# Two edits to a hybrid decoder layer on one core: when g's scale is copied, and when w_out's scale and first split are made

## The chip, the core and the metric

The kernel runs on one core of a Trainium2 chip. The metric is the device time of one launch in microseconds. Five engines work side by side, each through its own instructions in a fixed order: PE (matrix products; its weight loads are shown as PEld), DVE (VectorE), ACT (ScalarE), POOL (GpSimd) and SP, which here only issues transfers (DMA).

## What is computed

One layer (DEPTH 1, 1024 positions, width 1024) of a parallel-branch hybrid block:

```python
h = rms_norm(x, norm_mix_pre)
q, k, v, cb, cc, cx, g_att, g_conv = split(h @ w_in)
y_att  = stick_breaking_attention(q, k, v) @ w_att_branch     # 8 heads of 64
y_conv = (cb * causal_dwconv(cc * cx)) @ w_conv_branch
m = sigmoid(g_att) * y_att + sigmoid(g_conv) * y_conv
x = x + rms_norm(m @ w_out, norm_mix_post)
h = rms_norm(x, norm_ffn_pre)
a, g = split(causal_dwconv(h @ w_up))                          # width 2816 each
x = x + rms_norm((gelu(g) * a) @ w_down, norm_ffn_post)
```

## The kernel before

All products take float16 operands. A float32 tensor is scaled by a power of two and then split: ACT writes the rounded high part, DVE the remainder as the low part (`split`, L100: ACT at L102, DVE at L103). A product is then three passes on PE, high by high, high by low, low by high (PASSES, L38). The power of two for a weight comes from the sum of its squares: ACT squares each tile (`sumsq`, L62), DVE adds up the partial sums and rounds the total (L75, L76), PE adds over the partitions with a product by a matrix of ones (L81), and DVE makes the scale and its inverse by integer arithmetic on the exponent (L83 to L86). `scale_of` (L65) does all of this after the squares, and `wsplit` (L124) is `scale_of` followed by one `split` for each tile.

The work goes in stages: (1) the start, where x is normed, transposed and multiplied by w_v; (2) the attention, with the other input products filling PE's time beside it; (3) the branch products and seven blocks of gates, d = 1 to 7; (4) the product with w_out, with the second norm between its tiles; (5) the feed-forward part.

**The start** (L441 to L776) is ordered by hand-made means: jobs with costs in microseconds are handed to a planner (`Plan`, L2128), which simulates PE, ACT, DVE, POOL and SP with these costs and emits each engine's instructions in the order found. PE jobs marked `seq` keep the order in which they are written; other jobs go where the simulation has them ready. The jobs that matter here:
- The gain g of the first norm arrives as one row. DVE takes its maximum and a power of two from it (L476, L199 to L202) and rounds the pair (L481). PE spreads the row over the partitions in two halves (`gpb`, L496) and then the pair (`ps2`, L498). DVE copies the pair into `gs` (L500); its first entry is `s_h`, the scale of h.
- `norm_halves` (L511) norms a tile of 128 positions in two halves of 512 columns: squares on ACT (L514) and DVE (L516), small DVE operations (L518, L519), the power -1/2 on POOL (L521), then on DVE one product for each half (L523). It runs for tile 0 and for tile 1.
- On PE in written order: 4 products that only keep it busy (`warm`, L489), the transposes of tile 0 in two halves (L535), 2 more `warm`, two raw products of tile 0 with w_v (`v_raw`, L602, float32 without split, eight in all, k = 0 to 7), the transposes of tile 1 (`turn_pe(1)`, L543), the other six raw products.
- ACT scales the transposed tile 0 by `s_h` into `h32` (L711), which the raw products take; it also makes the high part of the transposed tile 1 (L725; the low part is DVE's L726) and squares w_v, whose scale is needed for its split (L729, L731). PE's product for that scale is L588.

**The gates** (L1281 to L1306): block d multiplies h by two columns of w_in, with seven half-size products in place of eight (`Gates`, a `Pair`, L2345). `prod(i)` (L2361) is 12 matrix products of 512 columns; three accumulators (banks a, b, c) take the seven, and each is evicted by ACT or DVE right after a `prod` (L2383). The written order of a block is `prod(1)`, the previous block's `prod(4)`, the preparation of the next block's weights, `merge_m` of the previous block (L1246), then `prod` 6, 5, 2, 7, 3, with `split_m` of the previous block behind 5. Stage 3 has no order by hand: the framework's scheduler goes through it with its own timing and takes for each engine the instruction that is ready and stands first in the program, evictions ahead.

At the end of block 5 the eight tiles of w_out are fetched and squared (`wfetch`, L1306). Behind the loop stand `gp[7].prod(4)` (L1307), `wsplit` for w_out (L1308), the merge and the split of block 7 (L1309, L1310). Raw tiles and split tiles of w_out, the `y` tiles of the branches, the gates' `ug`, and the split m of blocks 4 to 7 all come from one pool of 16 slots (`slab`, L251).

**The product with w_out** (`out_proj`, L1499; PE at L1510) starts with two tiles at once, k outermost: for each of the eight k it takes 2 tiles x 2 halves x 3 passes = 12 products. So w_out's tile k is needed 12 k products after the first. This stage and the feed-forward part are ordered by a second planner run (L1392), whose inputs the change does not touch.

Of the kernel before, what the change touches and what calls it, by code (L numbers as in the profile page):

```python
# [18 lines left out]
F32 = mybir.dt.float32  # L19
# [5 lines left out]
P = 128  # L25
T = 1024
D = 1024
KD = D // P
# [16 lines left out]
class Layer:  # L45
# [76 lines left out]
        return sm, st  # L122

    def wsplit(self, name, sm, st, pools=None):  # L124

        nc = self.nc
        wh, wht = (pools or (self.ws, "ws", self.wh, "wh"))[2:]
        s, inv = self.scale_of(sm, len(st), keep=len(st) > 1)
        out = []
        for i, t in enumerate(st):  # L130
            w = wh.tile([P, 2, D], F16, tag=wht, name=f"wh_{name}_{i}")
            if name[:2] in self.pool_split:
                nc.gpsimd.tensor_scalar(t, t, s, 0.0, ALU.mult, ALU.add)
                nc.scalar.activation(w[:, 0, :], t, AF.Copy)
                nc.gpsimd.tensor_tensor(w[:, 1, :], t, w[:, 0, :], ALU.subtract)
            else:
                self.split(w, t, s, f"{name}_{i}")
            out.append(w)
        return out, inv

    def wload(self, name, srcs, pools=None, after=None):
# [138 lines left out]
    def mixer(self, mid):  # L280
        tc, nc, a = self.tc, self.nc, self.a
        hT = self.hp.tile([P, 2, KD, T], F16, tag="hT", name="hT")
        with ExitStack() as ph1:
# [64 lines left out]
            with tc.tile_pool(name="ptp", bufs=2, space=bass.MemoryType.PSUM) as ptp:  # L348
# [75 lines left out]
                st = [self.ws.tile([P, D], F32, tag="ws", name=f"ws_v_{i}") for i in range(4)]  # L424
# [13 lines left out]
                gs = self.small("g_pre", keep=True)  # L438
                cst = self.small("cst", keep=True)
                inv_ov = cst[:, 1:2]  # L440
                with tc.manual_schedule(engines={ET.PE, ET.DVE, ET.Activation, ET.SP, ET.Pool}):  # L441
                    pl = Plan(dict(s=12, ws=4, wh=8, pm=3, pt=2, sm=8, rb=8, sc=16))
                    pl.own, pl.loaded = {"PE": 0.0}, 22.0
                    vec, act, pe, pool = nc.vector, nc.scalar, nc.tensor, nc.gpsimd
                    NOTE = lambda: Buf(None, lambda: {})

                    def given(p, tile, avail=0.0):
                        b = Buf(p, None)
                        b.tile, b.avail = tile, avail
                        pl.caps[p] -= 1  # L450
                        return b

                    def V(cost, fn, r, w, **kw):
                        return pl.add("V", cost, fn, r, w, **kw)

                    def A(cost, fn, r, w, **kw):
                        return pl.add("A", cost, fn, r, w, **kw)
# [9 lines left out]
                    raw_v = [given("ws", st[i], (6.1, 8.7, 10.0, 11.5)[i]) for i in range(4)]  # L467
                    sv = given("sm", self.small("sm_v"))
                    hb = [NOTE() for _ in range(8)]
                    jv = Buf("s", lambda: self.slot([P, D], F32, "jk_v_2"))  # L470
                    g_s, g_c, g_t = NOTE(), NOTE(), NOTE()
                    h0, h1 = slice(0, NH), slice(NH, D)
# [13 lines left out]
                    def warm(n):  # L486
                        def f():
                            for _ in range(n):
                                pe.matmul(wm.t, wz[:, :P], wz, start=True, stop=True)  # L489
                        M(0.43 * n, f, [zero], [wm])  # L490
# [3 lines left out]
                    ps2 = Buf("pm", lambda: pm.tile([P, NH], F32, tag="pm", name="g2"))  # L494
                    for c in range(2):
# [1 line left out]
                                                      gr[0:1, ds(c * NH, NH)], start=True, stop=True), [one_row, g_row], [(gpb, str(c))])  # L497
                    M(0.3, lambda: pe.matmul(ps2.t[:, 0:2], self.ones[0:1, :], g_c.t["g16"][0:1], start=True, stop=True),  # L498
                      [g_c], [ps2])
                    V(0.15, lambda: vec.tensor_copy(gs[:, 3:5], ps2.t[:, 0:2]), [ps2], [g_s])  # L500
                    def norm(tt):
                        r, x = Buf("sm", lambda: self.small(f"r_pre{tt}")), xs[tt]
                        A(1.25, lambda: self.sumsq(xt[tt], r.t[:, 0:1], f"n_pre{tt}"), [x], [r])
                        V(0.15, lambda: vec.tensor_scalar(r.t[:, 1:2], r.t[:, 0:1], 1.0 / D, EPS, ALU.mult, ALU.add), [], [r])
                        pl.add("G", 0.6, lambda: pool.tensor_tensor(r.t[:, 2:3], r.t[:, 1:2], self.neghalf, ALU.pow), [], [r])
                        g = gpb if tt < 2 else gbb
                        V(1.28, lambda: vec.scalar_tensor_tensor(
                            xt[tt], xt[tt], r.t[:, 2:3], g.t.rearrange("p k t -> p (k t)") if tt < 2 else gb,
                            ALU.mult, ALU.mult), [r, g], [x])

                    def norm_halves(tt):  # L511
                        r, x = Buf("sm", lambda: self.small(f"r_pre{tt}")), xs[tt]
                        lo, hi = xt[tt][:, :NH], xt[tt][:, NH:]
                        A(0.82, lambda: act.activation(self.junk(f"jk_n_pre{tt}")[:, :NH], lo, AF.Square, accum_out=r.t[:, 0:1]),  # L514
                          [(x, "0")], [(r, "0")])
                        V(0.76, lambda: vec.scalar_tensor_tensor(jv.t[:, :NH], hi, 1.0, hi, ALU.mult, ALU.mult,  # L516
                                                                 accum_out=r.t[:, 3:4]), [(x, "1")], [(r, "1"), jv])
                        V(0.15, lambda: vec.tensor_scalar(r.t[:, 4:5], r.t[:, 3:4], 1.0 / D, EPS, ALU.mult, ALU.add), [], [(r, "1")])  # L518
                        V(0.15, lambda: vec.scalar_tensor_tensor(r.t[:, 1:2], r.t[:, 0:1], 1.0 / D, r.t[:, 4:5], ALU.mult, ALU.add),  # L519
                          [(r, "0"), (r, "1")], [(r, "2")])  # L520
                        pl.add("G", 0.6, lambda: pool.tensor_tensor(r.t[:, 2:3], r.t[:, 1:2], self.neghalf, ALU.pow), [], [(r, "2")])  # L521
                        for c, sl in enumerate((slice(0, NH), slice(NH, D))):
                            V(0.66, lambda sl=sl: vec.scalar_tensor_tensor(  # L523
                                xt[tt][:, sl], xt[tt][:, sl], r.t[:, 2:3], gpb.t.rearrange("p k t -> p (k t)")[:, sl],
                                ALU.mult, ALU.mult), [(r, "2"), (gpb, str(c))], [(x, str(c))])

                    pt = {}

# [60 lines left out]
                        V(0.45, post, [ps], [b])  # L589
                        return b  # L590

                    h32 = Buf("s", lambda: self.slot([P, KD, P], F32, "h32"))
                    own = hT[:, :, :, :P]
                    pv = {}

                    def v_bank(tt):
                        pv[tt] = Buf("pm", lambda: pm.tile([P, NH], F32, tag="pm", name=f"pv{tt}"))
# [103 lines left out]
                        vec.tensor_scalar(cst[:, 1:2], inv_h, bv.t["inv"], 2.0 ** 15, ALU.mult, ALU.mult)  # L701

                    warm(4)
                    norm_halves(0)
                    turn_halves(0)
                    warm(2)
                    norm_halves(1)
                    v_bank(0)
                    square_v(0, 0, slice(0, D), "A")
                    for c in range(2):  # L710
# [6 lines left out]
                    square_v(3, 5, h1, "V")  # L717
                    bv = total("v", sv, lambda: sv.t, 6)
                    V(0.15, lambda: vec.tensor_scalar(vs0.t[:, 0:1], bv.t["s"], 2.0 ** -15, None, ALU.mult), [bv], [vs0])
                    for k in range(2):  # L720
                        v_raw(k)
                    turn_pe(1)
                    for k in range(2, KD):
                        v_raw(k)
                    A(1.1, lambda: act.activation(hT[:, 0, :, ds(P, P)], pt[1].t, AF.Copy, scale=s_h), [pt[1], g_s], [(hb[1], "0")])  # L725
                    V(1.27, lambda: vec.scalar_tensor_tensor(hT[:, 1, :, ds(P, P)], pt[1].t, s_h, hT[:, 0, :, ds(P, P)],  # L726
# [408 lines left out]
            with tc.manual_schedule(engines={ET.PE, ET.DVE, ET.Activation}):  # L1135
# [52 lines left out]
                for name, t in wtasks.items():  # L1188
                    if any(o.eng == "sum" for o in t.ops):
# [3 lines left out]
                        st = next(o.st for o in t.ops if o.st)  # L1193
# [17 lines left out]
        with ExitStack() as ph2:  # L1211
# [29 lines left out]
            def branches(*ds_, bi=1):  # L1241
                for d in ds_:
                    for _ in branch(bi, d, pm):
                        pass
# [9 lines left out]
            def split_m(d, m):  # L1254
                t = self.o16p.tile([P, 2, T], F16, tag="o16", name=f"m16_{d}") if d < 4 else \
                    self.slot([P, 2, T], F16, f"m16_{d}")
                self.split(t, m, s_m, f"m{d}")
                m16.append(t)
# [21 lines left out]
            wo_pools = (self.slab, "s", self.slab, "s")  # L1280
            for d in range(1, 8):  # L1281
                p = gp[d]
                p.prod(1)
                if d > 1:
                    gp[d - 1].prod(4)
                if d < 7:
                    self.pair_split(f"g{d + 1}")
                    self.pair_fetch(f"g{d + 2}" if d < 6 else "u0")
                if d > 1:
                    ms.append(merge_m(d - 1))  # L1290
                for i in (6, 5, 2, 7, 3):
                    p.prod(i)
                    if d >= 4 and i == 5:
                        split_m(d - 1, ms[d - 1])
                sig["gc", d], sig["ga", d] = p.ca, p.cg
                self.pair_sums(f"g{d + 2}" if d < 6 else "u0") if d < 7 else None
                if d < 3:
                    branches(5 + d)
                if d == 3:
                    nc.vector.tensor_scalar(smy, smy, 2.0, None, ALU.mult)  # L1300
                    s_m, inv_m = self.scale_of(smy, 16, keep=True)
                    for i in range(3):
                        split_m(i, ms[i])
                    self.dn_sums(GROUPS[0])
                if d == 5:
                    wo_raw = self.wfetch("wo", [a["w_out"][k] for k in range(8)], wo_pools, after=ms[4])  # L1306
            gp[7].prod(4)  # L1307
            wo, inv_wo = self.wsplit("wo", *wo_raw, wo_pools)  # L1308
            ms.append(merge_m(7))  # L1309
            split_m(7, ms[7])  # L1310
            self.mul(sgn[:, 24:25], inv_m, inv_wo)
# [1191 lines left out]
```

## Time and profile before

| what | value |
|---|---|
| median of 3 runs | 1299.8 us (1299.68 to 1301.29) |
| the profiled execution | 1300.07 us |
| its span, first to last instruction | 1298.4 us |
| PE busy | 1285.4 us, 99% |
| DVE, ACT busy | 1094.9 us (84%), 938.3 us (72%) |
| DMA | 131.53 MB, mean 101 GB/s |

The profile records one execution. Each row of its timeline is a start and a duration in us, the engine, the line of the kernel, the operation, what it writes and reads, and how many instructions were merged into it; in brackets stands how long the engine had been idle before it and which instruction ended that wait. A busy PE is counted from a start to a modelled end, and products overlap, so that the distance between starts says more than the durations. The launch's own time is 1.67 us longer than the span.

### The profile page before, as it was taken

The numbers are of one execution on the slowest core, as the hardware profiler recorded it, in microseconds if no ns is written. First come the engines' busy times: TensorE is split into PE (matmuls) and PEld (weight loads), VectorE is DVE, ScalarE is ACT, GpSimd is POOL, SyncE is SP. The second block draws the span as 40 slices with busy tenths as digits, with TensorE's granted clock in tenths as the row PEclk, the third lists the DMA queues.
The fourth block names the chain that finished last, engine by engine and source line by source line (L and its number), as shares of the span: only waits on it lengthen the run. The fifth ranks groups of instructions, "written<-read, shape, count | busy, mean of one in ns | idle before, by whom it ended". The sixth has DMA issues, their size and how long they took to land. (4 is left out here: it accounts for less than half of the span.)

```text
span 1298.4 us, 16904 instructions
## 1 busy us (share of the span) xinstructions
PE 1285.4 (99%) x6312; PEld 571.8 (44%) x6312; DVE 1094.9 (84%) x1764; ACT 938.3 (72%) x1333; POOL 83.5 (6%) x120
## 2 busy tenths in 40 slices
PE   9999999999999999999999999999999999999997
PEld 4444444444444444444444444444444444444443
DVE  7678888887878967877989999799879979979976
ACT  7578778777778964865566767877966877778534
POOL 2000000000000000000210000100300210120003
PEclk9999999999999999999999999999999999999999
DMA  7511111111101212250784312721951791394707
GB/s 262 131 34 49 49 34 33 34 33 33 49 1 49 65 65 68 95 195 34 182 224 122 114 50 81 274 67 17 202 171 33 126 247 49 60 235 156 199 1 130
DMA packets 68373, 131.53 MB, mean 101 GB/s; under 512 B 36913, under 2 KB 37041, under 8 KB 68290
## 3 DMA queue, kind: packets, MB, share of 16 engines
q1 hardware_dynamic: 57920, 93.74, 23.2%
q0 software_dynamic: 10368, 36.70, 13.7%
q8 instruction: 49, 0.80, 0.3%
q14 instruction: 34, 0.28, 0.1%
q10 hardware_dynamic: 2, 0.00, 0.0%
HBM read 84.52 MB, written 37.78 MB: 94 GB/s over the span
## 5 line engine op out<-in xcount | busy, mean ns | idle before, releaser
L1709 PEld LDWEIGHTS <-wh_u 128*128 128x128 f16 x1848 | 179.1, 98 | 218.3 <-issue 1.7
L2373 PEld LDWEIGHTS <-wh_g 128*128 128x128 f16 x588 | 57.0, 98 | 68.6
L1457 ACT ACTIVATE wh_u<-ws_u,sc_u 128x1024 f16<-128x1024 f32 (+1 forms) x66 | 66.4, 1007 | 28.3 <-DVE sc_u L1442 8.0
L1510 PE MATMUL py<-wh_wo,m 128*128 128x512 f16 x384 | 83.4, 379 | 1.0 <-DVE wh_wo L103 1.0
L1459 DVE SCALAR_TENSOR_TENSOR wh_u<-ws_u,sc_u,wh_u 128x1024 f16<-128x1024 f32 (+1 forms) x66 | 72.2, 1103 | 13.3 <-ACT wh_u L1457 12.6
L1872 ACT ACTIVATE st<-pq,sd 128x512 f32<-128x512 f32 x112 | 73.7, 697 | 10.0 <-DVE ua L1752 5.6
L1037 ACT ACTIVATE sh<-sp 128x1024 f16<-128x1024 f32 (+3 forms) x48 | 40.4, 842 | 52.3 <-DVE sp L1032 52.1
L1423 POOL DMA_DIRECT2D acc<-st x56 | 43.3, 772 | 427.5 <-ACT st L1872 427.5
L63 ACT ACTIVATE jk_u<-ws_u 128x1024 bf16<-128x1024 f32 x44 | 46.3, 1052 | 22.6 <-DMA ws_u<-w_up_nt 22.3
L1032 DVE TENSOR_TENSOR sp<-A,sp 1x1024 f32<-1x1024 f32 (+3 forms) x40 | 35.9, 897 | 30.0 <-PE A L994 27.4
L1510 PEld LDWEIGHTS <-m 128*128 128x128 f16 x384 | 37.4, 98 | 46.2 <-issue 1.6
L1041 DVE TENSOR_TENSOR sh<-sp,sh 128x1024 f16<-128x1024 f32 (+3 forms) x48 | 45.8, 954 | 13.5 <-ACT sh L1037 13.3
L1741 DVE SCALAR_TENSOR_TENSOR ua<-ca,cw_a,ua 128x1023 f32<-128x1023 f32 (+1 forms) x44 | 56.2, 1278 | 1.1 <-ACT ua L1739 1.1
L1741 DVE SCALAR_TENSOR_TENSOR ug<-cg,cw_g,ug 128x1023 f32<-128x1023 f32 (+1 forms) x44 | 56.2, 1276 | 0.1
L1067 DVE SCALAR_TENSOR_TENSOR w<-e,w 128x1024 f16<-128x1024 f32 (+3 forms) x48 | 45.7, 952 | 6.8 <-ACT w L1063 6.7
L1063 ACT ACTIVATE w<-e 128x1024 f16<-128x1024 f32 (+3 forms) x48 | 40.5, 843 | 14.7 <-DVE e L1058 13.7
L1058 DVE TENSOR_TENSOR e<-e,g 128x1024 f32<-128x1024 f32 (+3 forms) x48 | 45.7, 952 | 2.5 <-ACT g L1054 2.5
L1027 ACT ACTIVATE sp<-e,one 128x1024 f32<-128x1024 f32 (+3 forms) x48 | 44.4, 925 | 4.0 <-DVE e L1022 2.7
L1013 ACT ACTIVATE e<-z,cz 128x1024 f32<-128x1024 f32 (+3 forms) x48 | 43.0, 897 | 4.4 <-PE z L994 4.4
L216 PE MATMUL pcb<-hT,wh_cb 128*128 128x512 f16 x192 | 45.1, 380 | 0.0
L216 PE MATMUL pcx<-hT,wh_cx 128*128 128x512 f16 x192 | 44.9, 379 | 0.0
L216 PE MATMUL pcc<-hT,wh_cc 128*128 128x512 f16 x192 | 44.6, 380 | 0.0
(789 smaller groups left out, 2987.1 us busy)
## 6 DMA issues: line engine op xcount, KB each, us to landing
acc<-st POOLq DMA_DIRECT2D x56, 512.0 KB, 5.9
ws_u<-w_up_nt SPq DMA_DIRECT2D x44, 512.0 KB
ds<-w_down SPq DMA_DIRECT2D x22, 512.0 KB
ws_g<-w_in_nt SPq DMA_DIRECT2D x14, 512.0 KB
x<-x SPq DMA_DIRECT2D x8, 512.0 KB
ws_wo<-w_out SPq DMA_DIRECT2D x8, 512.0 KB
xr<-x SPq DMA_DIRECT2D x8, 512.0 KB
yacc<-acc SPq DMA_DIRECT2D x16, 256.0 KB
```

Of the source, the lines that this page charges most:

```text
L63: self.nc.scalar.activation(self.junk(f"jk_{name}"), src, AF.Square, accum_out=acc)
L216: nc.tensor.matmul(ps, w[:, wi, ds(k * P, P)], hT[:, hi, k, ds(c * NH, NH)], start=n == 0, stop=n == last)
L1041: nc.vector.tensor_tensor(sh[:, 1, :, off:], u["sp"][:, :, off:], sh[:, 0, :, off:], ALU.subtract)
L1058: nc.vector.tensor_tensor(e[:, :, off:], e[:, :, off:], u["g"][:, :, off:], ALU.mult)
L1067: nc.vector.scalar_tensor_tensor(w[:, 1, :, off:], u["e"][:, :, off:], 2.0 ** 14, w[:, 0, :, off:], ALU.mult, ALU.subtract)
L1457: A(C["As" if big else "Ash"], lambda: act.activation(dst.t[:, 0, dsl], src.t[:, ssl], AF.Copy, scale=sb.t["s"]), [(src, sreg), sb], [(dst ...
L1459: V(C["V" if big else "Vh"], lambda: vec.scalar_tensor_tensor(dst.t[:, 1, dsl], src.t[:, ssl], sb.t["s"], dst.t[:, 0, dsl], ALU.mult, ALU. ...
L1510: pe.matmul(b.t, m16[k].t[:, h_, ds(tt * P, P)], wo[k].t[:, w_, sl], start=k == 0 and p == 0, stop=k == 7 and p == 2)
L1709: pe.matmul(b.t, p.w[wt].t[:, wi, ds(wc * NH + k * P, P)], pr.block(i, h, k), start=first and n == 0, stop=n == 3 * KH - 1, skip_group_che ...
L1741: V(C["V"], lambda lag=lag: vec.scalar_tensor_tensor(u.t[:, lag:], c.t[:, :T - lag], sm.t[:, 2 - lag:3 - lag], u.t[:, lag:], ALU.mult, ALU ...
L1872: A(C["Ah"], lambda tt=tt, b=b, st=st: act.activation(st.t[:, tt % 2, :], b.t, AF.Copy, scale=q.sd.t[:, 0:1]), [b, q.sd], [(st, str(tt % 2 ...
L2373: nc.tensor.matmul(ps, w[wt][:, wi, ds(wc * NH + k * P, P)], self.block(i, hi, k), start=first and n == 0, stop=n == 3 * KH - 1, skip_grou ...
```

## The change

At the start: the DVE copy of the pair into `gs` leaves its place ahead of tile 0's norm and goes between the two half products of that norm; it now also waits for the first of them. Three raw products instead of two stand ahead of `turn_pe(1)`. `norm_halves` gets arguments for further waits, which are passed empty, and the buffer `h32` is declared earlier.

At w_out: `wsplit` becomes a generator `wsplits` that stops after each tile. In block 7, behind `prod(6)`, its first step is taken: the whole of `scale_of` and the split of w_out's tile 0. The other seven splits stay where they were, behind `gp[7].prod(4)`.

```diff
@@ wsplit
+        steps = self.wsplits(name, sm, st, pools)
+        while True:
+            try:
+                next(steps)
+            except StopIteration as got:
+                return got.value
+
+    def wsplits(self, name, sm, st, pools=None):
...
             out.append(w)
+            yield
         return out, inv
@@ mixer, the start
-                    V(0.15, lambda: vec.tensor_copy(gs[:, 3:5], ps2.t[:, 0:2]), [ps2], [g_s])
...
-                    def norm_halves(tt):
+                    def norm_halves(tt, first=(), prior=(), then=None):
...
                             V(0.66, lambda sl=sl: vec.scalar_tensor_tensor(
                                 xt[tt][:, sl], xt[tt][:, sl], r.t[:, 2:3], gpb.t.rearrange("p k t -> p (k t)")[:, sl],
                                 ALU.mult, ALU.mult), [(r, "2"), (gpb, str(c))], [(x, str(c))])
+                            if then and c == 0:
+                                then(x)
...
-                    norm_halves(0)
+                    norm_halves(0, then=lambda x: V(0.15, lambda: vec.tensor_copy(gs[:, 3:5], ps2.t[:, 0:2]), [ps2, (x, "0")], [g_s]))
...
-                    for k in range(2):
+                    for k in range(3):
                         v_raw(k)
                     turn_pe(1)
-                    for k in range(2, KD):
+                    for k in range(3, KD):
                         v_raw(k)
@@ mixer, the gates
                     if d >= 4 and i == 5:
                         split_m(d - 1, ms[d - 1])
+                    if d == 7 and i == 6:
+                        steps = self.wsplits("wo", *wo_raw, wo_pools)
+                        for _ in range(1):
+                            next(steps)
...
             gp[7].prod(4)
-            wo, inv_wo = self.wsplit("wo", *wo_raw, wo_pools)
+            try:
+                while True:
+                    next(steps)
+            except StopIteration as got:
+                wo, inv_wo = got.value
```

More of the change, by code (lines that the diff above doesn't have):

```diff
@@ L469, in mixer @@
                     hb = [NOTE() for _ in range(8)]
+                    h32 = Buf("s", lambda: self.slot([P, KD, P], F32, "h32"))
                     jv = Buf("s", lambda: self.slot([P, D], F32, "jk_v_2"))
@@ L514, in norm_halves @@
                         A(0.82, lambda: act.activation(self.junk(f"jk_n_pre{tt}")[:, :NH], lo, AF.Square, accum_out=r.t[:, 0:1]),
-                          [(x, "0")], [(r, "0")])
+                          [(x, "0"), *first], [(r, "0")])
                         V(0.76, lambda: vec.scalar_tensor_tensor(jv.t[:, :NH], hi, 1.0, hi, ALU.mult, ALU.mult,
-                                                                 accum_out=r.t[:, 3:4]), [(x, "1")], [(r, "1"), jv])
+                                                                 accum_out=r.t[:, 3:4]), [(x, "1"), *prior], [(r, "1"), jv])
                         V(0.15, lambda: vec.tensor_scalar(r.t[:, 4:5], r.t[:, 3:4], 1.0 / D, EPS, ALU.mult, ALU.add), [], [(r, "1")])
@@ L590, in total @@
                         return b
-                    h32 = Buf("s", lambda: self.slot([P, KD, P], F32, "h32"))
                     own = hT[:, :, :, :P]
@@ L703, in mixer @@
                     warm(4)
-                    norm_halves(0)
+                    norm_halves(0, then=lambda x: V(0.15, lambda: vec.tensor_copy(gs[:, 3:5], ps2.t[:, 0:2]), [ps2, (x, "0")], [g_s]))
                     turn_halves(0)
                     warm(2)
-                    norm_halves(1)
+                    norm_halves(1, (), ())
                     v_bank(0)
```

## The prediction

> **What bounds the kernel now.** I read the page's busy times first, then PE's waits by line, then the timeline at the two places that the change touches.
>
> ```profile
> span 1298.4 us, 16904 instructions
> PE 1285.4 (99%) x6312; PEld 571.8 (44%) x6312; DVE 1094.9 (84%) x1764; ACT 938.3 (72%) x1333; POOL 83.5 (6%) x120
> ...
> PE py L1510 <- DVE wh_wo L103: 1.0, 1, 1.0
> ```
>
> PE is busy in 99% of the span and idle for 1298.4 - 1285.4 = 13.0 us. Neither edit takes a product away, so only waits can be won, and one in PE's list of waits (in all, times, longest) is what the change names: 1.0 us before `py` (L1510), for w_out's split. The start's part does not show as a wait, since there PE is kept busy by `warm` products. The total at stake is near 0.1% of the time.
>
> **The change at w_out.**
>
> ```profile
> 577.62 0.15 DVE L76 CAST rb<-sc 128x1 bf16<-128x1 f32 x1
> ...
> 589.81 2.75 PE L2373 MATMUL pg7c<-hT,wh_g 128*128 128x512 f16 x12
> 592.40 0.17 PE L81 MATMUL pr<-rb,ones 128*128 128x1 bf16 x1
> 592.43 2.75 PE L2373 MATMUL pg7b<-hT,wh_g 128*128 128x512 f16 x12
> ...
> 593.96 2.17 ACT L102 ACTIVATE wh_wo<-ws_wo,sc 128x1024 f16<-128x1024 f32 x2
> 595.14 0.38 PE L1510 MATMUL py<-wh_wo,m 128*128 128x512 f16 x1
> 595.23 1.28 DVE L103 SCALAR_TENSOR_TENSOR wh_wo<-ws_wo,sc,wh_wo 128x1024 f16<-128x1024 f32 x1
> 596.55 15.70 PE L1510 MATMUL py<-wh_wo,m 128*128 128x512 f16 x72 [1.04 <-DVE wh_wo L103]
> 597.02 2.47 DVE L103 SCALAR_TENSOR_TENSOR wh_wo<-ws_wo,sc,wh_wo 128x1024 f16<-128x1024 f32 x2
> ```
>
> The sum of squares is rounded at 577.77, but its product `pr` comes at 592.40, behind nearly all of block 7. From there runs a chain: DVE's scale, ACT's high part to 595.1 (593.96, and 1.15 for one of two), DVE's low part from 595.23 to 596.51, and PE's second `py` product at 596.55. Twelve products take 2.59 us (589.81 to 592.40), 0.216 each. Without the wait the first `py` would start at 592.43 + 2.59 = 595.02 and the second at 595.24. So the loss is 596.55 - 595.24 = **1.31 us**; the 1.04 of the wait view is less because the first product's modelled end reaches into it.
>
> After the change `pr` stands behind `prod(6)` of block 7. The last instructions of `prod(6)` (bank b, from `hB`) are the second row here; the first are older products:
>
> ```profile
> 574.92 2.75 PE L2373 MATMUL pg6c<-hT,wh_g 128*128 128x512 f16 x12
> ...
> 581.18 1.03 PE L2373 MATMUL pg7b<-hB,wh_g 128*128 128x512 f16 x4
> ...
> 583.98 0.72 ACT L2415 ACTIVATE cgg<-cgg,sc_g 128x512 f32<-128x512 f32 x1 [2.25 <-DVE cgg L2402]
> 584.83 0.60 ACT L2393 ACTIVATE ugg<-pg7c 128x512 f32<-128x512 f32 x1
> 585.99 1.23 DVE L1251 TENSOR_TENSOR ywa<-ywa,ywc 128x1024 f32<-128x1024 f32 x1
> ```
>
> It ends at 581.18 + 4 x 0.216 = 582.04, and `pr` runs there, 4.3 us after its input; it keeps its 0.03 us of PE. The scale is three DVE operations, 0.4 us together as the three like L76's size go; the split takes ACT 1.15 and DVE 1.28. They move into a stretch where ACT has a hole of 2.25 us before 583.98, and should be done by 589, 6 us before PE asks. What they push back there are evictions and the merge of block 6: by up to 1.28 + 0.4 = 1.7 us. ug's eviction (584.83 to 585.43) has until the next product in its bank at 589.81, 4.4 us, so PE doesn't feel it. The split also takes a slot: by my count of the slab 15 of 16 are held then, so `ug` may wait for the slot that L1251 frees at 587.2. That still leaves 2 us.
>
> What is late next is w_out's tile 1, needed 13 products after the first, at 595.02 + 13 x 0.216 = 597.83. If nothing of it moved, its low part would end at 597.02 + 1.28 = 598.30, a wait of 0.5 us. But DVE is relieved of tile 0's 1.28 us and of the scale just ahead of it, so I take about 597.0 and no wait. Tile 2 has 2.6 us more and so on. **1.3 us** gained; both ends 0.8 and 1.3.
>
> Does it last? At the next stage every engine waits for PE. The first row is of the windows view (busy time and instructions of PE, PEld, DVE, ACT and POOL, the granted clock, the DMA share, GB/s):
>
> ```profile
> 592.00:612.00 20.00, 18.96 (x89) 8.46 (x88) 15.98 (x18) 11.62 (x12) 0.00 (x0) 1.00 0.00 0
> ...
> 612.52 0.17 PE L1445 MATMUL pr_u<-rb_u,ones 128*128 128x1 bf16 x1
> 612.73 0.16 DVE L1440 TENSOR_SCALAR sc_u<-pr_u 128x1 int32<-128x1 int32 x1 [3.80 <-PE pr_u L1445]
> 613.11 1.15 ACT L1457 ACTIVATE wh_u<-ws_u,sc_u 128x1024 f16<-128x1024 f32 x1 [6.58 <-DVE sc_u L1442]
> ```
>
> DVE idles 3.80 us and ACT 6.58 us until PE's product at 612.52, no transfer runs from 592 to 612, and the order behind is the second planner's, unchanged. So the rest moves forward as one block, with its own waits at L1709 as they are.
>
> **The change at the start.**
>
> ```profile
> 5.87 0.15 DVE L518 TENSOR_SCALAR r_pre<-r_pre 128x1 f32<-128x1 f32 x1
> ...
> 7.63 1.89 PE L489 MATMUL warm<-wz 128*128 128x512 f16 x4
> 7.77 0.16 DVE L500 COPY g_pre<-g 128x2 f32<-128x2 f32 x1 [1.75 <-PE g L498]
> 8.17 0.55 POOL L521 TENSOR_TENSOR r_pre<-r_pre,neghalf 128x1 f32<-128x1 f32 x1 [4.78 <-DVE r_pre L519]
> 8.76 1.41 DVE L523 SCALAR_TENSOR_TENSOR x<-x,r_pre,g_ps 128x512 f32<-128x512 f32 x2 [0.74 <-POOL r_pre L521]
> 8.89 0.63 PE L489 MATMUL warm<-wz 128*128 128x512 f16 x1
> 9.56 1.11 PE L535 MATMUL pt_pre0a<-ident,x 128*128 128x128 f32 x4
> ...
> 10.71 0.69 ACT L711 ACTIVATE h<-pt_pre0a,g_pre 128x512 f32<-128x512 f32 x1 [1.78 <-PE pt_pre0a L535]
> 11.09 0.59 PE L489 MATMUL warm<-wz 128*128 128x512 f16 x2
> 11.52 1.92 PE L602 MATMUL pv<-ws_v,h 128*128 128x512 f32 x4
> ```
>
> DVE sits 1.75 us before the copy, and behind the copy stand L519, POOL's power and both half products. Moved, L519 follows L518 to about 6.15, and 0.74 later, the power between them, comes the first half product, near 6.9; the copy stays at 7.77, held by PE's product, and the second half product follows near 7.9. The norm is 1.9 us earlier. But PE's four `warm` products last until 8.89 + 0.42 = 9.31 (three steps of 0.42 from 7.63), so the transposes come at 9.31 instead of 9.56: **0.25 us**, and ACT's `h32` with them.
>
> ```profile
> 12.00:16.00 4.00, 4.00 (x18) 2.18 (x17) 3.09 (x9) 3.91 (x9) 0.03 (x1) 1.00 0.98 366
> ...
> 14.14 1.88 PE L602 MATMUL pv<-ws_v,h 128*128 128x512 f32 x4
> 15.61 1.09 ACT L725 ACTIVATE hT<-pt_pre,g_pre 128x1024 f16<-128x1024 f32 x1
> 15.86 0.17 PE L588 MATMUL pr_v<-rb_v,ones 128*128 128x1 bf16 x1
> ...
> 25.84 3.19 PE L613 MATMUL pv<-wh_v,hT 128*128 128x512 f16 x14 [0.22 <-DVE hT L736]
> ```
>
> A raw product is two instructions 0.43 apart (14.14 to 15.86 for four), so the third one ahead of the transposes puts these 0.86 us later, done near 15.1; ACT wants them at 15.61 - 0.25. No loss, no gain. `pr_v`, behind the fourth raw product, comes 0.1 to 0.15 earlier. From `h32` on ACT has next to no gap (3.91 of 4.00 us in the first row, of the windows view), and the next PE wait (25.84, L736) hangs on ACT and DVE, so it moves by what they move, 0.15 to 0.25. I take **0.2 us**. Ends: 0.7 lost if `pr_v` falls behind one more raw product (0.86 less 0.15); 0.8 more gained if PE's rate doubled before the four `warm` products (4 x 0.21).
>
> PE runs at two rates here: the four are 0.42 apart, the two at 11.09 reach the raw product at 11.52, 0.21 apart, though the profile page shows the granted clock as full all through. [...]
>
> **The sum** is 1.31 + 0.2 = 1.5 us. From the profiled execution's 1300.07 that gives 1298.6; it stands 0.27 above the median, so from 1299.8 it is **1298.3 us**, 0.12% less.
>
> **Rivals.**
> - *Nothing moves at w_out.* The scheduler leaves `pr` late, as it left it 14.6 us after its input. For: PE takes gates' products first whenever ready. Against: its written place is now ahead of five of them. Only 0.2 remains: 1299.6.
> - *Handed on.* Tile 1 or 2 of w_out is late: 0.5 us back, 1298.8. For: ACT's and DVE's work is the same, and slots are short. Against: DVE has 1.7 us less to do there.
> - *Slower: PE waits at `pr`.* The sum is rounded at 577.77 in the trace. If the scheduler's own timing has it earlier and puts `pr` ahead of the 574.92 row, PE stands 577.77 - 574.92 = 2.9 us, and the time is 1298.3 + 2.9 = 1301.2. It decides from 1.5 us of wait, that is, if `pr` comes before 576.3. Against: `prod(6)` stands ahead of it and ends at 582.04. [...]
> - *The rate's border moves.* If it falls before the `warm` four, 0.8 more is gained: 1297.5. If it falls two raw products later, these four instructions take 0.86 each instead of 0.43, 1.7 us more: 1300.0.
>
> **How the numbers follow.** Forecast 0.58, own range 1297.7 to 1298.9; nothing moves 0.12; handed on 0.14; wait at `pr` 0.08; rate 0.08. The runs before spread from 1299.68 to 1301.29, so I let the range go from 1297.3 to 1300.3: it holds all but the slower case and tails. 0.2%, about what a measurement of this kernel can tell from no change, is 2.6 us. Faster than that needs a second gain of 1.1 us, 0.07; slower needs a new wait of 4.1 us, 0.05; the rest, 0.88, is within.
>
> **What would show it.** Right: `pr` (L81, the one for w_out) near 582, its split before 590, no wait before `py`, the second `py` 0.22 behind the first, and the rows of L1709 earlier by one common amount. At the start: L519 near 6.0 with no wait for L498 ahead of it, L535 near 9.3, L613's wait near 25.6. Wrong: a new PE wait in L2373 between 574 and 592, a wait at `py` for a later tile, or `h32` not before 10.7.

## The result, and the profile after

The changed kernel takes 1298.89 us in the median of 22 runs (1297.87 to 1300.03), the kernel before, run beside it, 1300.63 us (1299.68 to 1301.40). The ratio is 0.9986, 95% interval 0.998 to 0.9992: 1.74 us less between the medians. The forecast was 1298.3 us, 1.5 us less than 1299.8; its range, 1297.3 to 1300.3, held the time.

The profiled execution of after took 1299.48 us, with a span of 1297.8 us. First from its page: the span, the busy times, and then all that is left in PE's list of waits (in all, times, longest).

```profile
span 1297.8 us, 16905 instructions
...
PE 1286.0 (99%) x6312; PEld 572.6 (44%) x6312; DVE 1095.0 (84%) x1764; ACT 938.6 (72%) x1333; POOL 84.6 (7%) x120
...
PE warm L499 <- DVE wz L362: 1.7, 1, 1.7
PE pu2a L1727 <- ACT cg L1736: 1.2, 1, 1.2
PE pu0b L1727 <- DVE ca L1733: 1.1, 1, 1.1
PE pu2a L1727 <- ACT ca L1742: 0.3, 1, 0.3
```

The wait at `py` is gone, so is one of 0.2 us at `pv` (L613), and no other has come into the list; lines after the start stand 10 to 18 further down than in the kernel before. The timeline of after around w_out (start, duration, engine, line, operation):

```profile
581.84 1.03 PE L2391 MATMUL pg7b<-hB,wh_g 128*128 128x512 f16 x4
582.71 0.17 PE L81 MATMUL pr<-rb,ones 128*128 128x1 bf16 x1
...
585.03 0.15 DVE L83 TENSOR_SCALAR sc<-pr 128x1 int32<-128x1 int32 x1
...
586.63 1.15 ACT L102 ACTIVATE wh_wo<-ws_wo,sc 128x1024 f16<-128x1024 f32 x1 [1.36 <-DVE sc L85]
587.81 1.28 DVE L103 SCALAR_TENSOR_TENSOR wh_wo<-ws_wo,sc,wh_wo 128x1024 f16<-128x1024 f32 x1
587.88 0.60 ACT L2411 ACTIVATE ugg<-pg7c 128x512 f32<-128x512 f32 x1
...
590.50 0.38 PE L1528 MATMUL py<-wh_wo,m 128*128 128x512 f16 x1
590.72 2.75 PE L2391 MATMUL pg7c<-hT,wh_g 128*128 128x512 f16 x12
593.31 2.32 PE L1528 MATMUL py<-wh_wo,m 128*128 128x512 f16 x10
595.46 2.75 PE L2391 MATMUL pg7b<-hT,wh_g 128*128 128x512 f16 x12
598.05 13.98 PE L1528 MATMUL py<-wh_wo,m 128*128 128x512 f16 x64
...
611.87 0.17 PE L1463 MATMUL pr_u<-rb_u,ones 128*128 128x1 bf16 x1
```

`pr` stands at 582.71, right behind the four products that end `prod(6)`, and the low part is done at 589.09, as forecast. Because tile 0 is there so early, eleven `py` products were taken into block 7, one at 590.50 and ten at 593.31, between the gates' last products. From the four products into pg7b to `pr_u` it was 612.52 - 581.18 = 31.34 us before; now it is 611.87 - 581.84 = 30.03: **1.31 us** less. The row of the windows view for the stretch before `pr_u` agrees: PE is busy in all 20.00 us (18.96 before).

```profile
592.00:612.00 20.00, 20.00 (x95) 9.14 (x94) 15.42 (x15) 10.32 (x11) 0.00 (x0) 1.00 0.00 0
```

But the four products came 0.66 us later than before (581.84 against 581.18). The start of after shows why:

```profile
3.92 3.78 PE L506 MATMUL g_ps<-g_row,on 1*128 1x512 f32 x4
...
7.63 1.89 PE L499 MATMUL warm<-wz 128*128 128x512 f16 x4
7.82 1.41 DVE L532 SCALAR_TENSOR_TENSOR x<-x,r_pre,g_ps 128x512 f32<-128x512 f32 x2 [2.19 <-PE g L508]
9.14 0.15 DVE L714 COPY g_pre<-g 128x2 f32<-128x2 f32 x1
9.32 1.06 PE L546 MATMUL pt_pre0a<-ident,x 128*128 128x128 f32 x4
10.41 0.69 ACT L721 ACTIVATE h<-pt_pre0a,g_pre 128x512 f32<-128x512 f32 x1 [1.79 <-PE pt_pre0a L546]
11.02 1.06 PE L499 MATMUL warm<-wz 128*128 128x512 f16 x2
11.88 3.27 PE L612 MATMUL pv<-ws_v,h 128*128 128x512 f32 x6
14.98 1.04 PE L554 MATMUL pt_pre<-ident,x 128*128 128x128 f32 x8
```

The transposes start 0.24 us earlier (9.32 against 9.56), but the two `warm` products at 11.02 are still 0.43 apart (0.21 in before), and the six raw instructions take 14.98 - 11.88 = 3.10 us instead of 6 x 0.43 = 2.58. PE went over to its full rate later in this launch. The trace records that moment: 10.83 us in before's profile, 12.94 in after's (6 x 0.43, and 0.43 more for each raw instruction at half rate, puts it near 12.9 too). The first two raw instructions start 0.85 apart (11.88 and 12.73), those from 13.27 on 0.43, so the same work takes twice the time at the first rate, and this costs about (12.94 - 10.83) / 2 = 1.05 us; 0.39 of it is made up within the start, and 0.66 is left.

### The profile page after: what moved, and what is told of

Its sections match the earlier page's. It is cut to its first block, busy times and chain, and to the rows that moved or that the text cites. A ratio compares the mean times of both kernels' runs of the same rounds, so it can differ in the third digit from the quotient of the medians.

```text
span 1297.8 us, 16905 instructions
## 1 busy us (share of the span) xinstructions
PE 1286.0 (99%) x6312; PEld 572.6 (44%) x6312; DVE 1095.0 (84%) x1764; ACT 938.6 (72%) x1333; POOL 84.6 (7%) x120
```

## The experiments

Each kernel was timed in rounds against the kernel before. The mean differences with one standard error are worked out from the single times. The 14 profiles (two of them before and after) were laid product by product over that of before. **PE's products shift rigidly, within 0.02 us, except in four places**: the start, a transposed load near 47 us, the w_out part, and waits from 669 to 706 us. The table takes the shifts apart (us; minus is earlier). "Rate" is when PE's full rate begins. "Start" is the shift of the first product of `v` that stands at 46.62 in before, less half of (rate - 10.83). "Loads" is what comes on from there to 66 us, "w_out" from 560 to 640, "late" from 640 to 706; the sum is all four and the half of the rate.

| kernel | rate | start | loads | w_out | late | sum | timed mean against before |
|---|---|---|---|---|---|---|---|
| before | 10.83 | 0 | 0 | 0 | 0 | 0 | 0 |
| before again | 12.23 | -0.05 | 0.36 | 0 | 0.79 | 1.82 | +0.06 ± 0.21 |
| w_out part | 12.99 | -0.25 | 0.63 | -1.32 | 0.16 | 0.31 | -1.52 ± 0.17 |
| w_out again | 13.73 | -0.25 | 0.32 | -1.32 | -0.10 | 0.11 | -1.36 ± 0.19 |
| start part | 10.35 | -0.06 | 0 | 0 | -0.25 | -0.55 | -1.33 ± 0.22 |
| start again | 12.60 | -0.39 | 0 | 0 | 0.10 | 0.59 | -1.01 ± 0.29 |
| copy alone | 11.51 | -0.36 | 0.34 | 0 | -0.89 | -0.57 | -1.28 ± 0.20 |
| raw alone | 11.41 | -0.01 | 0 | 0 | -0.42 | -0.14 | -1.17 ± 0.17 |
| after | 12.94 | -0.39 | 0 | -1.32 | 0.07 | -0.58 | -1.78 ± 0.18 |
| after again | 11.49 | -0.35 | 0 | -1.32 | -0.17 | -1.50 | -2.74 ± 0.13 |
| step first | 13.00 | -0.39 | 0 | -0.58 | -0.56 | -0.45 | -1.91 ± 0.16 |
| three splits | 11.33 | -0.27 | 0 | -1.32 | 0.59 | -0.74 | -2.44 ± 0.26 |
| no two `warm` | 11.34 | 0.07 | 1.38 | -1.32 | 0.16 | 0.55 | -0.55 ± 0.27 |
| no four `warm` | 12.87 | -0.72 | 0.20 | -1.32 | -0.21 | -1.02 | -1.51 ± 0.26 |

A profile is one launch, so its sum holds that launch's rate and loads; the timed mean is over 10 or 11 launches (after: 22).

### The w_out part alone

The start of before, with block 7's step as in after:

```diff
+                    if d == 7 and i == 6:
+                        steps = self.wsplits("wo", *wo_raw, wo_pools)
+                        for _ in range(1):
+                            next(steps)
```

> The w_out part alone, with the start of before. Theory 1 (the whole gain is the 1.31 us that PE lost at the product py; it reaches the end undiminished): PE's wait at py is gone, pr stands near 582 us between the products into pg7b and pg7c, and the mean time is 1.2 to 1.4 us below before's (ratio about 0.9990). Rival (the w_out part is partly handed on and the start gives the rest): 0.3 to 0.9 us below. Rival (PE waits at pr now, or the pulled-in py products cost something): 0 or slower.

Measured: 1300.06 us against 1301.67, ratio 0.9987 (0.9979 to 0.9996). The w_out column is -1.32 in this profile and in nearly every other that has the part, whatever came before. So theory 1 holds here: the forecast's 1.31 us, neither handed on nor more (timed: 1.52 ± 0.17).

### The start part alone

```diff
-                    V(0.15, lambda: vec.tensor_copy(gs[:, 3:5], ps2.t[:, 0:2]), [ps2], [g_s])
...
-                    norm_halves(0)
+                    norm_halves(0, then=lambda x: V(0.15, lambda: vec.tensor_copy(gs[:, 3:5], ps2.t[:, 0:2]), [ps2, (x, "0")], [g_s]))
...
-                    for k in range(2):
+                    for k in range(3):
```

> The start part alone (copy of g's scale behind the first half product, three raw products first), with before's end. Theory 1: the transposes into ptA start 0.24 us earlier and that is the whole gain, 0.2 to 0.4 us (ratio about 0.9998); PE's loss of 1.3 us at py near 596 stays. Rival (the start is worth most of the 1.7 us between the medians): 0.8 to 1.2 us below. Rival (the third raw product delays pr_v and its evictions): 0.4 to 0.7 us slower.

Measured: 1300.49 against 1301.67, ratio 0.999 (0.9981 to 0.9999). The transposes are at 9.31 and the wait at `py` is there, as theory 1 said; but 1.3 us is near the size that the rival gave. The next two take it apart.

### The copy alone, and three raw products alone

The first has only the first two edits of the diff above, the second only the last.

> Only the copy of g's scale is moved, with two raw products first as before. Theory 1: transposes into ptA near 9.3 us instead of 9.56, 0.2 to 0.4 us faster. Rival (the copy's place changes nothing, because the half products wait for PE's pair product and not for ACT): 0.0 us. If the third raw product is what gains, this one equals before.

> Only the number of raw products ahead of pr_v is changed, from two to three; the copy stays in its old place. Theory 1: no difference, within 0.2 us of before (pr_v comes one product of 0.43 us later, but VectorE and ScalarE have slack there). Rival (pr_v is what ScalarE's and VectorE's later evictions wait for): 0.4 to 0.7 us slower. Rival (PE waits for something after the second raw product that the third now covers): 0.4 us faster.

Measured: copy 1300.20, ratio 0.9991 (0.9982 to 1.0); raw 1300.47, ratio 0.9991 (0.9982 to 1.0), both against 1301.67. Each alone timed as much as both together, and theory 1 (0.2 to 0.4 us, and no difference) was too low for both. Three raw products alone can't have sped the start: the transposes stand at 9.56 and `start` is -0.01. What the two have in common lies behind the start. The planner, given jobs a little earlier or later, finds another order: with three raw products, with or without the copy, from 29.5 us on, with the copy alone a different one from 16.5 us on. In both the transposed loads of x (`hT<-x`, L554 before) are issued in another order among the other transfers. Behind 51 us all five engines have before's order again, in every kernel with the start's edits alone. SP's queue in before and in three raw alone (for SP: start, and the time to the end of the last one in the row), and the products that need them:

```profile
42.08 0.36 SPq L798 DMA_DIRECT2D ws_cx<-w_in_nt  x1
42.78 3.06 SPq L554 DMA_TRANSPOSE hT<-x  x2
...
46.62 4.05 PE L414 MATMUL pv<-wh_v,hT 128*128 128x512 f16 x18
```

```profile
39.78 2.75 SPq L566 DMA_TRANSPOSE hT<-x  x2
43.42 6.75 SPq L566 DMA_TRANSPOSE hT<-x  x5
...
46.90 4.05 PE L423 MATMUL pv<-wh_v,hT 128*128 128x512 f16 x18
```

PE asks for the last load of its next tile with the third product of this row, 0.43 behind its start. In the old order that is the first load of the pair at 42.78, in three raw alone the first of the five. The trace's record of landings has it at 46.90 in before, 0.15 us ahead of the need (46.62 + 0.43 = 47.05), and in the three other launches of the old order 0.19 (before again), 0.27 and 0.50 us behind it (w_out, twice). In three raw alone it lands at 46.65, 0.68 ahead of 47.33. Of the ten launches of a new order seven have it 0.42 to 0.74 ahead; copy alone 0.13 behind, the kernel without the four `warm` even with it, the one without the two 1.33 behind. Behind time, it is a wait of PE, as in the w_out part (third row):

```profile
44.01 3.32 SPq L566 DMA_TRANSPOSE hT<-x  x2
...
47.45 0.59 PE L423 MATMUL pv<-wh_v,hT 128*128 128x512 f16 x2
48.43 3.63 PE L423 MATMUL pv<-wh_v,hT 128*128 128x512 f16 x16 [0.38 <-DMA hT<-x]
```

From issue to landing this load took 4.12 to 4.37 us in the four launches of the old order and 3.18 to 3.34 us in the ten others. So one thing that the start's edits bring, in most launches, is slack for this load. In before `ws_cx`, 512 KB, is issued 0.7 us ahead of it, in the three other launches of the old order 0.45 us, in the new ones more than 7 us ahead or behind; whether that holds the load up was not tried.

### The step at the head of block 7

The step goes ahead of the block's `prod(1)`, its first instruction, so it passes `prod(1)`, the previous block's `prod(4)` and `merge_m`, and `prod(6)`:

```diff
+                if d == 7:
+                    steps = self.wsplits("wo", *wo_raw, wo_pools)
+                    for _ in range(1):
+                        next(steps)
                 p.prod(1)
...
-                    if d == 7 and i == 6:
```

> As after, but the step with w_out's scale stands one place earlier, so that pr is queued some 2 to 3 us earlier among block 7's products. Theory 1 (pr's place matters only in that it comes before py by more than the 4.1 us of its chain): same as after, within 0.2 us. Rival (pr put earlier makes PE wait for the cast or the buffer that pr needs): 0.3 to 1.5 us slower than after, with a wait of PE at pr in the list.

Measured: 1299.60 against 1301.20, ratio 0.9987 (0.9978 to 0.9996). The timeline of PE:

```profile
581.44 0.17 PE L81 MATMUL pr<-rb,ones 128*128 128x1 bf16 x1
...
585.35 0.38 PE L1528 MATMUL py<-wh_wo,m 128*128 128x512 f16 x1
586.30 1.24 PE L1528 MATMUL py<-wh_wo,m 128*128 128x512 f16 x5 [0.57 <-DVE wh_wo L103]
```

Neither theory holds. PE has no wait at `pr`, which came 1.27 us earlier than in after, but the scheduler now took `py` products as far up as 585.35, and the second of them waits 0.57 us for the low part. Behind it stands a product of block 7 into bank a (587.38) whose bank had been evicted at 585.42. From the matching products the part is worth 0.58 us instead of 1.32; the timed mean is 0.83 above that of after again, and 0.13 below the first one of after.

### Three splits instead of one

```diff
-                        for _ in range(1):
+                        for _ in range(3):
```

> As after, but three splits of w_out instead of one are made inside the last block's gates. Theory 1 (after has no wait left at py, so there is nothing to win): within 0.2 us of after. Rival (a second tile of w_out comes late in after and costs a few tenths): 0.2 to 0.5 us faster than after. Rival (two more splits on ScalarE and VectorE inside block 7 delay its gates): 0.3 to 1 us slower.

Measured: 1299.16 against 1301.20, ratio 0.9979 (0.997 to 0.9988), on the chip where after again (below) stands at 0.9979 as well. The w_out column is -1.32 again: nothing was left there to win, and the two splits harm no gate.

### Without the two, and without the four `warm` products

One line is left out in each, `warm(2)` or `warm(4)` (the products' results are not used).

> As after, without the two warm products between the transposes and the first raw product. Theory 1 (PE waits there for the copies of ptA anyway): the raw products start at the same time, 0 to 0.2 us faster. Rival (they keep PE's rate rising): PE's full rate begins later, 0.5 to 1 us slower.

> As after, without the four warm products ahead of the transposes into ptA. Theory 1 (these products end the chain that sets the transposes' start at 9.32 us): the transposes start 0.3 to 0.8 us earlier, and the end comes 0.3 to 0.8 us earlier. Rival (the transposes then wait for what the four products hid, the landing of their operands): 0. Rival (without them PE's full rate begins later): 0.5 to 1 us slower.

Measured: without the two 1300.96, ratio 0.9998 (0.9989 to 1.0007); without the four 1300.08, ratio 0.9989 (0.998 to 0.9998); before 1301.20. Without the two (first fence) the raw products start earlier, but the planner now puts `pr_v` behind five raw products (ten instructions) instead of four, so that it comes at 16.50; after again, with its rate change 0.15 later, has it at 16.00. The low part of tile 2 is late, and PE waits 0.75 us for it. The late load near 47 us cost 1.21 more. The full rate began at 11.34, so this launch shows nothing of the rival that the two keep the rate rising.

```profile
11.15 2.92 PE L612 MATMUL pv<-ws_v,h 128*128 128x512 f32 x6
...
14.78 1.88 PE L612 MATMUL pv<-ws_v,h 128*128 128x512 f32 x4
16.50 0.17 PE L599 MATMUL pr_v<-rb_v,ones 128*128 128x1 bf16 x1
...
26.16 3.20 PE L623 MATMUL pv<-wh_v,hT 128*128 128x512 f16 x14 [0.75 <-DVE hT L745]
```

Without the four (second fence) the transposes do start 0.70 earlier, held now by DVE's half products, and the start column is 0.33 better than after's.

```profile
7.82 1.41 DVE L532 SCALAR_TENSOR_TENSOR x<-x,r_pre,g_ps 128x512 f32<-128x512 f32 x2 [2.10 <-PE g L508]
8.62 1.12 PE L546 MATMUL pt_pre0a<-ident,x 128*128 128x128 f32 x4 [0.92 <-DVE x L532]
```

The timed mean doesn't show it: it is 1.2 us above that of after again, on the same chip. Why is open; the one profile has nothing that costs so much. The rival that the full rate begins later without the four is not excluded: it began at 12.87 in this launch, within the range of the other kernels (10.35 to 13.73). So the four set the transposes' time, as the prediction had it, and no version here is shown to beat after.

### Before, after and both parts once more

All four kernels in one set of rounds, unchanged, to see whether each build has an offset of its own.

> The kernel before once more, built and loaded anew, nothing changed. The four single parts measured so far lay 1.2 to 1.6 us below before, although their profiles, put on an equal start of PE's full rate, differ from before's by 0 (three raw products alone) to 1.3 us (w_out part). Theory 1 (the parts are what the profiles show, the rest is the spread of launches: where PE's full rate begins, and whether a transposed load is slow): within 0.3 us of before. Theory 3 (every build and load of a kernel has an offset of its own, so that a difference of 1 us between two builds means little): off by 0.5 to 1.5 us, to either side.

> The kernel after once more, built and loaded anew. Theory 1: 1.6 to 1.9 us below before, 0.2 to 0.5 us below the w_out part alone. Theory 3: anywhere from 0.7 to 2.7 us below. In the profile: PE has no wait at py, pr_u of the first block of the last stage comes 30.03 us after the third product group into pg7b.

> The w_out part alone once more. Theory 1: 1.2 to 1.6 us below before, 0.2 to 0.5 us above after. Theory 3: another value than the first time (1.6 below) by 0.5 us or more.

> The start part alone once more. Theory 1: 0.2 to 0.5 us below before and 1.2 to 1.4 us above after. The rival that the start, with the other order that the planner then chooses from 24 us on, is worth 1 us or more on average: 1.0 to 1.4 us below before again, and then after is not the sum of its parts. Theory 3: another value than the first time (1.2 below) by 0.5 us or more.

Measured against 1301.67: before again 1301.32, ratio 1.0001 (0.9992 to 1.0011); after again 1298.62, ratio 0.9979 (0.997 to 0.9988); w_out again 1300.07, ratio 0.9991 (0.9982 to 1.0); start again 1300.37, ratio 0.9993 (0.9984 to 1.0002). Theory 3 finds no support in before, itself within 0.06 ± 0.21, nor in the parts, which repeat within 0.16 and 0.32. But after went from -1.78 ± 0.18 to -2.74 ± 0.13, by 0.96 ± 0.22 and past the 1.6 to 1.9 of theory 1, so an offset of single builds or measurements is not excluded. Within this set the parts add up: -1.36 - 1.01 = -2.37 ± 0.35 against -2.74 ± 0.13. The first pair, -1.52 - 1.33 = -2.85 ± 0.28, doesn't fit the first -1.78. Theory 1's price for the start falls: the start timed about 1.0 to 1.3 us, not 0.2 to 0.5. The last rival was right on the size; that the sum would fail doesn't show in this set.

Before again shows the fourth place. ACT's rows, first of before again, then of three raw alone: ACT waits for a load of `ws_u`, and behind that stands `ca`, which PE needs near 692.

```profile
691.97 1.06 ACT L63 ACTIVATE jk_u<-ws_u 128x1024 bf16<-128x1024 f32 x1 [1.07 <-DMA ws_u<-w_up_nt]
...
693.02 0.58 ACT L1724 ACTIVATE ca<-pu0a 128x512 f32<-128x512 f32 x1
```

```profile
690.01 1.06 ACT L63 ACTIVATE jk_u<-ws_u 128x1024 bf16<-128x1024 f32 x1 [0.42 <-DMA ws_u<-w_up_nt]
...
691.06 0.58 ACT L1735 ACTIVATE ca<-pu0a 128x512 f32<-128x512 f32 x1
```

With the wait of 1.07 PE loses 0.5 us at `pu2a` here, with 0.42 nothing.

**What the start's part is made of.** The means over the four profiles with before's start (before twice, w_out twice) and the six with an edit there (start twice, copy, raw, after twice): start -0.14 and -0.26, loads 0.33 and 0.06, late 0.21 and -0.26, rate 12.45 and 11.72. The differences are -0.12, -0.27, -0.47 and, by half, -0.36: 1.2 us, as timed. Of these the direct gain and the load have a cause that the traces show; for three raw alone that is the load only, some 0.3 of the 1.17 that it timed. The late waits and the rate vary from launch to launch by more than their difference, and the late waits come where, with the start's edits alone, every engine's order is that of before. So whether these two shares are the edits' doing or chance of ten launches stays open, and with them some 0.8 us of the 1.2. So does why after gains 1.78 ± 0.18 in one measurement and 2.74 ± 0.13 in the other.

## Why the prediction was right, and where not

- **w_out, 1.31 us: right** in place and size (1.31 to 1.32 in every profile with the step behind `prod(6)`). `pr` came at 582.71 (near 582 was said), the split before 590, and all behind `pr_u` moved as one block as far as the waits near 690.
- *The second `py` 0.22 behind the first* was not foreseen rightly: the scheduler took eleven `py` products into block 7. It cost nothing here; with the step at the head of the block the same freedom cost 0.57 us.
- *Handed on, nothing moves, PE waits at `pr`*: none came. ug's eviction went from 584.83 to 587.88. Less the 0.66 of the launch that is 2.39 us, more than the 1.7 said, but within the 4.4 that it had.
- **First half product near 6.9: wrong.** I gave it the norm as its only condition (POOL's power was done at 6.34). It also takes the spread gain, of which PE tells once, behind the last of its four products, at 7.71 (L506 at 3.92, 3.78 long); the row names the pair's product L508, which tells on the same semaphore at 7.75, and the trace doesn't separate the two. The half product came at 7.82, 0.94 us earlier than before and not 1.9, with the copy behind both halves at 9.14. It changed little, since the four `warm` products last until 9.31, as the prediction had it: transposes 0.24 us earlier, where 0.25 was said.
- **The start's 0.2 us: the direct gain is right, the term is mis-sized.** Directly it is 0.06 us (the start part against before, with rate changes at 10.35 and 10.83) or 0.14 (after against w_out, 0.39 less 0.25, both with a late rate change) to 0.35 (after again against raw alone, with a rate change near 11.45). PE's wait of 0.22 us at 25.84 (L613), from which the term was read, doesn't move to 25.6: after and after again don't have it, the start part has. The failed step is "No loss, no gain" for the third raw product. In the start itself it holds (-0.01 in three raw alone), but it takes for granted that the order beyond the start stays. Either edit changes the planner's order up to 51 us, and the start's part timed 1.0 to 1.3 us, of which the traces explain some 0.4.
- *The rate's border* was a rival with ends of 1297.5 and 1300.0; no row of before showed that it moves. It stood elsewhere in each of the 14 launches profiled (10.83 and 12.23 in the two profiles of before, 12.94 and 11.49 in those of after; 10.35 to 13.73 in all), and hid the start's gain in after's profile; whether the change shifts it on average is open.
- The total was right because w_out's term carried it: 1.5 us said, 1.78 ± 0.18 measured. That the first measurement came so near is partly luck: taken off 1299.8, the 2.74 ± 0.13 of the second gives 1297.06, below the range's lower end of 1297.3.

## What to carry to other kernels

The chain from a product to a split was hidden with the product 7.79 us ahead of its user in PE's order (582.71 to 590.50, the split done at 589.09); with the product 1.27 us further up, in the one try here, a free scheduler had room to pull the user up into a new wait of 0.57 us. An edit to a planner's input can change the order far behind the edit, here up to 51 us: compare the orders, and look for loads with no slack there. A difference of 1 us in a kernel of 1300 is read from many launches and from products matched between traces, after the launch's own terms are taken out.

## What the runs showed of the hardware

PE's full rate began between 10.35 and 13.73 us in the 14 traces, a spread of 3.38, and lasted 1283.41 us in ten and 1280.00 in four, two lengths 3.41 us apart. Half of the spread of 3.38, 1.7 us, is as much as the launches of before vary in the first measurement (1299.68 to 1301.40); those of after again vary by 0.79 us only (1298.39 to 1299.18), so the spread need not show in full in ten or so launches. The granted clock of the windows view shows 1.00 all the same (7.40 to 9.50 in before, where the four `warm` products are 0.42 apart); only the spacing of the products, and the moment that the trace records, tell.

The transposed loads that one line issues don't take SP one time. The row of copy alone (for ten of them: shortest, median, longest in ns) has 1.23 to 2.66 us:

```profile
L565 SPq DMA_TRANSPOSE hT<-x x10: 1232/1291/2658, 25.8 to 49.3; - x10
```
